# The last two column groups of an encoder block's second MLP product: written order on TensorE in place of the scheduler's

## The chip, the cores and the metric

The kernel runs on one core of a Trainium2 chip. The metric is the device time of one execution in microseconds (us); less is better. Before the change the median of 3 runs is 1791.88 us (1791.26 to 1792.47).

## What is computed

One encoder block on x (256 tokens by 2048 channels), all in float32: two gated branches (chunked gated linear attention and a Hyena convolution), an output projection, a layer norm, then an MLP and a second layer norm. The change touches the MLP's end only:

```python
    h = _layernorm(DEEPNORM_ALPHA * h + mix, ln1_g[l], ln1_b[l])
    ff = jnp.square(jax.nn.relu(h @ w_ff1[l])) @ w_ff2[l]
    h = _layernorm(DEEPNORM_ALPHA * h + ff, ln2_g[l], ln2_b[l])
```

## The kernel before

**Products.** Every float32 operand is split into a high part (rounded to fp32r by ScalarE) and a low part (the remainder, by VectorE: `split_hi_lo`, L89 to L91). A product is three matmuls: high by high, high by low, low by high (L201 to L203 for 512 columns, L969 to L971 for 256). Weights come from DRAM as blocks of 1 MB, `raw`, three buffers; a block is split in two halves of 128x1024.

**The end of the MLP.** The tokens are two blocks of 128, tb 0 and 1; the 2048 output columns are four groups of 512. `ff_pairs` has done most of the k range by another scheme; its sums lie in `z1`. What is left are 10 k tiles (5 half blocks of weights) for each of the 4 column groups and both token blocks, and these run here (from L1373 on):

- Groups 0 and 1: both token blocks together, a half block at a time (w2_30_0 to w2_31_1).
- Group 2 (`left`, PSUM tiles w2_32_0 and w2_32_1) and group 3: their ten half blocks are kept resident, so that token block 0 can go through both groups first and token block 1 afterwards. The first two halves (`kept`) come through the usual buffers, whi and wlo; the other eight are fetched by `resident_pieces` (four loads on L924) into tiles that have come free, in this order: xh_r, xl_r, fraw_r, fa, and four halves of wr3.
- The code writes: 30 products w2_32_0 (tb 0, group 2), 30 products w2_33_0 (tb 0, group 3), then 30 products w2_32_1 (tb 1, group 2), then group 3 of tb 1 in two PSUM tiles of 256 columns, w2_33_10 and w2_33_11, 30 products each.
- `add_ff` (L1360) takes a finished PSUM tile in on VectorE: add to z1 (L1362), two statistics (L1364), and for tb 1 also a multiplication by the gain (L1366).
- After w2_33_0, token block 0 is normed: statistics, `norm_scale`, two chunks on VectorE (L1431, L1441), two on ScalarE (L1433), gain and bias (L1445, L1449), and its four stores on SP (L1418).
- Token block 1's norm is partly done on TensorE: z1 is split (`split_z`, tiles whiz and wloz, the first 1024 columns ahead, 512 more later), multiplied by a unit matrix into PSUM (L1457, six matmuls), and when the last statistics are known (L1463) a diagonal of minus the mean is multiplied with the gain onto it (L1475); then VectorE scales it (L1479) and four stores go out on SP and one on ScalarE's queue.

**Who sets the order.** Instructions of one engine run in the order of its queue. A scheduler that simulates the program in time sets that order from the written program, unless an instruction was handed to `tc.keep_in_program_order`, which puts those instructions of an engine behind one another as written. Before the change that holds for the `ff_pairs` stage (through `pin`) and for VectorE's work from L1440 on and the L1457 matmuls, but not for the products of groups 2 and 3, nor for the splits of the resident blocks.

Of the kernel before, what the change touches and what calls it, by code (L numbers as in the profile page):

```python
# [20 lines left out]
KT = D // P  # L21
# [26 lines left out]
def block_kernel(  # L48
# [25 lines left out]
    nc = tc.nc  # L74
    MM = nc.tensor.matmul

    base = ctx.enter_context(tc.tile_pool(name="base", bufs=1))
# [5 lines left out]
    def psum_main(name):  # L83
        return mmp.tile([P, 512], F32, tag="mm", name=name)
# [4 lines left out]
    def split_hi_lo(hi, lo, src):  # L89
        return (nc.scalar.copy(hi, src),  # L90
                nc.vector.tensor_tensor(lo, src, hi.bitcast(F32), op=ALU.subtract))  # L91
# [20 lines left out]
    def weight_half(n, h):  # L112
        return (wp.tile([P, D // 2], F32R, tag="whi", bufs=3, name=f"whi{n}_{h}"),
                wp.tile([P, D // 2], F32R, tag="wlo", bufs=3, name=f"wlo{n}_{h}"))
# [21 lines left out]
    def next_block():  # L136
        fetch()
        return queue.popleft()
# [50 lines left out]
        for h in range(n, 2):  # L189
            channel_products(ps, act, parts[h], range(8 * h, 8 * h + 8))  # L190

    def token_half(pss, act, half, tbs, kt0, ends=(0, KT - 1)):
        hi, lo = half
        for j in range(2):
            kt = kt0 + j
            wh = hi[:, j * 512:(j + 1) * 512]
            wl = lo[:, j * 512:(j + 1) * 512]
            for tb in tbs:
                sh = act[:, kt, 0, tb * P:(tb + 1) * P]
                sl = act[:, kt, 1, tb * P:(tb + 1) * P]  # L200
                MM(pss[tb], sh, wh, start=(kt == ends[0]), stop=False)  # L201
                MM(pss[tb], sh, wl, start=False, stop=False)  # L202
                MM(pss[tb], sl, wh, start=False, stop=(kt == ends[1]))  # L203

    def token_products(pss, act, blocks, tbs, b0):
        for b, parts in enumerate(blocks):
# [3 lines left out]
    def token_group(act, name):  # L210
        pss = [psum_main(f"{name}_{tb}") for tb in range(NT)]
        for b in range(4):
            token_products(pss, act, [next_block()], range(NT), b)
            pump()
        return pss
# [17 lines left out]
    ident = base.tile([P, P], F32, tag="ident", name="ident")  # L233

    def act_tile(pool, tag, name):
        return pool.tile([P, KT, 2, L], F32R, tag=tag, name=name)
# [5 lines left out]
    dfth = base.tile([P, 4, P], F32R, tag="dfth", name="dfth")  # L242
# [13 lines left out]
    with tc.tile_pool(name="xp", bufs=1) as xp, tc.tile_pool(name="xq", bufs=1) as xq:  # L256
# [44 lines left out]
        for k0, n in PIECES:  # L301
            raw = pieces[k0]
# [12 lines left out]
            if k0 == 0:  # L315
                hi, lo = places[0]
# [165 lines left out]
    for i in range(2 * NCH):  # L482
        c, o = divmod(i, 2)
# [217 lines left out]
    for g in range(4):  # L701
        pss = token_group(xT, f"g1_{g}")
# [168 lines left out]
    for g in range(4):  # L871
        pss = token_group(xT, f"g2_{g}")
# [20 lines left out]
    for g in range(4):  # L893
        pss = token_group(yhT, f"ho{g}")
# [11 lines left out]
    ep = ctx.enter_context(tc.tile_pool(name="ep", bufs=1))  # L906
# [4 lines left out]
    def load_rows(i0):  # L911
        rows = zr[:, 2:4]
        for i in range(2):
            nc.scalar.dma_start(rows[:, i, :], ln_rows[i0 + i:i0 + i + 1, :].broadcast_to([P, D]))
        return rows

    tc.keep_in_program_order(nc.scalar.preload_act_table_set("natural_log_exp_and_others"))

    def resident_pieces(parts):
        for part in parts:  # L920
            n = fetched[0]
            fetched[0] = n + 1
            raw = wp.tile([P, D], F32, tag="raw", bufs=3, name=f"raw{n}")
            nc.sync.dma_start(raw, wblk[n])  # L924
            for h, (hi, lo) in enumerate(part):
                split_hi_lo(hi, lo, raw[:, h * 1024:(h + 1) * 1024])
        return parts

    def resident(slots):
        return resident_pieces([[(hi[:, c:c + 1024], lo[:, c:c + 1024]) for c in (0, 1024)] for hi, lo in slots])  # L930

    def halves(pool, tag, name):
        t = pool.tile([P, 4, D], F32R, tag=tag, name=name)
        return [(t[:, 0], t[:, 1]), (t[:, 2], t[:, 3])]
# [22 lines left out]
        if tb == 0:  # L957
            biased[0] = nc.vector.tensor_tensor(zc, zc, rows[:, 1, at:at + n], op=ALU.add)

    def column_half(pss, act, half, ch, tbs, kt0, ends=(0, KT - 1)):  # L960
        hi, lo = half
        for j in range(2):
            kt = kt0 + j
            cs = slice(j * 512 + ch * 256, j * 512 + ch * 256 + 256)
            for tb in tbs:
                ps = pss[tb][ch][:, 0:256]
                sh = act[:, kt, 0, tb * P:(tb + 1) * P]
                sl = act[:, kt, 1, tb * P:(tb + 1) * P]
                MM(ps, sh, hi[:, cs], start=(kt == ends[0]), stop=False)  # L969
                MM(ps, sh, lo[:, cs], start=False, stop=False)  # L970
                MM(ps, sl, hi[:, cs], start=False, stop=(kt == ends[1]))  # L971

    def column_products(pss, act, blocks, tbs, b0):
        for ch in range(2):
# [9 lines left out]
    for i, t in ((0, turn_b), (1, turn_i)):  # L984
        raw = ep.tile([P, 1024], F32, tag="wx", name=f"turn{i}")[:, 0:512].rearrange("p (a b) -> p a b", b=P)
# [11 lines left out]
    for g in range(3):  # L997
        pss = token_group(mT, f"wo{g}")
# [3 lines left out]
    parts = resident([x0] + halves(ep, "f", "wr1"))  # L1002
    pss = [[psum_main(f"wo3_{tb}{ch}") for ch in range(2)] for tb in range(NT)]
    column_products(pss, mT, [queue.popleft()], range(NT), 0)
    stop_at[0] = FF_PAIRS
    hT = act_tile(ep, "hT", "hT")
# [342 lines left out]
    def ff_close(pss, joins):  # L1349
        form_products(pss, SLOTS - 1, 2, (5, 6))  # L1350
        take_sums(pss, SLOTS - 1, (5, 6))
        for s in range(SLOTS, SLOTS + 8):
            if s in FORMED:
                forms(FORMED[s])
        for j in joins + join_sums(1):
            j()
# [3 lines left out]
    def add_ff(ps, tb, at, n, last=False, order=lambda ins: ins):  # L1360
        zc = z1[:, tb, at:at + n]
        order(nc.vector.tensor_tensor(zc, zc, ps, op=ALU.add))  # L1362
        for i in range(n // 256):
            order(nc.vector.bn_stats(st2[:, tb, at // 256 + i, :], zc[:, i * 256:(i + 1) * 256]))  # L1364
        if tb and not last:
            order(nc.vector.tensor_tensor(zc, zc, rows2[:, 0, at:at + n], op=ALU.mult))  # L1366
# [5 lines left out]
    f3 = Rest()  # L1372
    ENDS = (SLOTS, D_FF // P - 1)  # L1373
# [3 lines left out]
    def next_half():  # L1377
        if not ready:
            ready.extend(next_block())
        return ready.popleft()  # L1380

    for g in range(2):
        pss = [psum_main(f"w2_3{g}_{tb}") for tb in range(NT)]
        for i, kt in enumerate(at_kt):
            token_half(pss, f3, next_half(), range(NT), kt, ENDS)
            if g == 0 and i == 1:
                ff_close(*open_sums)
                rows2 = load_rows(2)
        for tb in range(NT):
            add_ff(pss[tb], tb, g * 512, 512)  # L1390
    left = [psum_main(f"w2_32_{tb}") for tb in range(NT)]
    kept = [next_half() for _ in at_kt[:2]]

    def quarters(*tiles):
        at = [t[:, k:k + 1024] for t in tiles for k in range(0, t.shape[1], 1024)]
        return [[(at[0], at[1]), (at[2], at[3])], [(at[4], at[5]), (at[6], at[7])]]
# [2 lines left out]
    own = [ep.tile([P, n], F32R, tag=t, name=f"{t}_r")  # L1399
           for t, n in (("xh", D), ("xl", D), ("fraw", D))]  # L1400
    parts = resident_pieces(quarters(*own, *spare)
                            + [[(a[:, c:c + 1024], b[:, c:c + 1024]) for c in (0, 1024)] for a, b in halves(ep, "hT", "wr3")])
    parts = [half for block in parts for half in block]
    third, fourth = list(zip(kept + parts[:3], at_kt)), list(zip(parts[3:], at_kt))
    diagonal = base.tile([P, 2, P], F32, tag="as", name="diagonal")
    minus = diagonal[:, 0]
    nc.vector.tensor_scalar(minus, ident, -1.0, None, op0=ALU.mult)
    unit = base.tile([P, 4, P], F32R, tag="dfth", name="unit")[:, 0]
    nc.scalar.copy(unit, ident)
    zg = [weight_half("z", h) for h in range(2)]  # L1410

    def split_z(h, n):
        return split_hi_lo(zg[h][0][:, 0:n], zg[h][1][:, 0:n], z1[:, 1, h * 1024:h * 1024 + n])[1]

    split_z(0, 1024)

    def store(tb, at, n, queue=nc.sync):
        queue.dma_start(out[tb * P:(tb + 1) * P, at:at + n], z1[:, tb, at:at + n])  # L1418

    ps = psum_main("w2_33_0")  # L1420
    for half, kt in third:
        token_half(left, f3, half, [0], kt, ENDS)
    add_ff(left[0], 0, 1024, 512)
    for half, kt in fourth:
        token_half([ps], f3, half, [0], kt, ENDS)
    pss = [psum_main(f"w2_33_1{ch}") for ch in range(2)]
    add_ff(ps, 0, 1536, 512)
    rs, nb = norm_scale(st2, 0, "2")
# [3 lines left out]
    for at, zc, wg, wb in chunks[2:]:  # L1432
        nc.scalar.activation(zc, zc, AF.Identity, scale=rs, bias=nb)  # L1433
    for half, kt in third:
        token_half(left, f3, half, [1], kt, ENDS)
    for ch in range(2):
        for half, kt in fourth:
            column_half([None, pss], f3, half, ch, [1], kt, ENDS)
    keep = tc.keep_in_program_order
    for at, zc, wg, wb in chunks[:2]:  # L1440
        keep(nc.vector.scalar_tensor_tensor(zc, zc, rs, wb, op0=ALU.mult, op1=ALU.add))  # L1441
        store(0, at, 512)
# [35 lines left out]
    for at, n in CENTRED:  # L1478
        nc.vector.scalar_tensor_tensor(z1[:, 1, at:at + n], po[at][:, 0:n], rs, rows2[:, 1, at:at + n],  # L1479
                                       op0=ALU.mult, op1=ALU.add)  # L1480
# [146 lines left out]
```

## Time and profile before

| what | value |
|---|---|
| median of the runs | 1791.88 us |
| the profiled execution's own time | 1790.62 us |
| its span (first to last instruction) | 1788.8 us |
| TensorE matmul busy | 1778.7 us (99%) |
| VectorE busy | 1472.7 us (82%) |
| ScalarE busy | 1050.2 us (59%) |
| granted TensorE clock, mean | 0.999 |

The times below are us from the start of the span. PE is TensorE (PEld its weight loads), DVE VectorE, ACT ScalarE, POOL GpSimd, SP the queue that issues most DMAs. A row of the timeline has start, duration, engine, line, operation, output<-input, and in brackets the idle time of the engine ahead of it with what ended it. The profile leaves out buffer numbers: w2_32_0, w2_33_0 and the others are all `w`, so they are told apart by the order of the queue. Matmuls overlap: a product of 512 columns shows 0.39 us, but the next one starts before it ends.

### The profile page before, as it was taken

Reading aid. Unit: us, or ns where it says so; the run is one execution under the profiler, and the core shown is the slowest. Engines: PE = TensorE matmul, PEld = TensorE weight load, DVE = VectorE, ACT = ScalarE, POOL = GpSimd, SP = SyncE. Lnnn points to the kernel's source line nnn. Section 1 sums busy time; section 2 is a strip of 40 time slices with the busy share of each in tenths; the row PEclk is TensorE's granted clock in tenths of the full one; section 3 lists DMA queues with packets and bytes.
Section 4 is the critical chain, followed back from the end, with each engine's and each line's share of the span. In section 5 each row is a group of like instructions: output and inputs, shape, how many; then the busy total and the mean of one; then the engine's idle time right before and its main releaser. Section 6 shows DMA issues by size and latency. Waiting matters only on the chain.

```text
span 1788.8 us, 23484 instructions
## 1 busy us (share of the span) xinstructions
PE 1778.7 (99%) x8751; PEld 1502.3 (84%) x8751; DVE 1472.7 (82%) x1901; ACT 1050.2 (59%) x1414; POOL 176.9 (10%) x230
## 2 busy tenths in 40 slices
PE   9999999999999999999999999999999999999998
PEld 7888888888888888888888889888888888888886
DVE  6789886885679998998755558889989999999997
ACT  6678777875344444444544446666666666666653
POOL 1011110000011211111000000011111111111100
PEclk9999999999999999999999999999999999999999
DMA  8668775455797979798555674678888888888863
GB/s 320 240 241 294 255 239 200 147 168 203 234 291 244 293 238 289 256 295 259 210 190 183 247 265 153 236 215 267 250 250 253 265 244 265 247 252 254 265 217 135
DMA packets 81010, 427.90 MB, mean 239 GB/s; under 512 B 10008, under 2 KB 12584, under 8 KB 40192
## 3 DMA queue, kind: packets, MB, share of 16 engines
q1 hardware_dynamic: 47664, 336.35, 51.2%
q0 software_dynamic: 26032, 70.13, 19.2%
q10 hardware_dynamic: 7200, 19.93, 3.1%
q8 instruction: 68, 1.11, 0.3%
q14 instruction: 46, 0.38, 0.1%
HBM read 383.43 MB, written 16.25 MB: 223 GB/s over the span
## 4 chain that ended last, share of the span: by engine, by line
PE 98%; DVE 1%; DMA 0%; issue 0%; ACT 0%; SPq 0%; DVEq 0%
PE f L151 13%; PE f L155 7%; PE w L1264 5%; PE w L1266 5%; PE w L1265 5%; PE g L202 3%; PE g L201 3%; PE g L203 3%; PE ux L202 3%; PE ux L203 3%; PE ux L201 3%; PE r L201 2%; PE r L202 2%; PE r L203 2%; PE k L151 2%; PE v L201 2%
## 5 line engine op out<-in xcount | busy, mean ns | idle before, releaser
L90 ACT CAST whi<-raw 128x1024 fp32r<-128x1024 f32 x368 | 387.6, 1055 | 388.4 <-PE ux L203 92.0
L91 DVE TENSOR_TENSOR wlo<-raw,whi 128x1024 fp32r<-128x1024 f32 x368 | 448.3, 1222 | 186.5 <-ACT whi L90 183.4
L151 PE MATMUL f<-hT,whi 128*128 128x512 f32 x984 | 243.6, 391 | 0.0
L151 PEld LDWEIGHTS f<-hT,whi 128*128 128x128 f32 x984 | 180.8, 188 | 35.0
L1122 DVE TENSOR_TENSOR wlo<-fraw,whi 128x1024 fp32r<-128x1024 f32 x108 | 132.0, 1222 | 14.9 <-ACT whi L1125 11.8
L155 PEld LDWEIGHTS f<-hT,wlo 128*128 128x128 f32 x984 | 126.2, 191 | 4.7
L155 PE MATMUL f<-hT,wlo 128*128 128x256 f32 x984 | 127.7, 283 | 0.0
L1125 ACT CAST whi<-ring 128x1024 fp32r<-128x1024 f32 x54 | 56.9, 1054 | 107.0 <-DVE ring L1122 107.0
L1185 POOL DMA_DIRECT2D ring<-wblk x54 | 47.0, 870 | 715.4 <-DVE ring L1122 715.4
L1125 ACT CAST whi<-fraw 128x1024 fp32r<-128x1024 f32 x108 | 113.5, 1051 | 0.1
L202 PE MATMUL g<-wlo,xT 128*128 128x512 f32 x256 | 100.1, 391 | 0.0
L203 PE MATMUL ux<-whi,xT 128*128 128x512 f32 x256 | 99.9, 390 | 0.0
L1125 ACT CAST b_h<-ring 128x1024 fp32r<-128x1024 f32 x108 | 84.9, 835 | 25.5 <-PE w L1266 24.9
L203 PE MATMUL g<-whi,xT 128*128 128x512 f32 x256 | 99.8, 390 | 0.0
L202 PE MATMUL ux<-wlo,xT 128*128 128x512 f32 x256 | 99.6, 389 | 0.0
L201 PE MATMUL g<-whi,xT 128*128 128x512 f32 x256 | 93.8, 392 | 0.0
L201 PE MATMUL ux<-whi,xT 128*128 128x512 f32 x256 | 89.7, 389 | 0.0
L1122 DVE TENSOR_TENSOR b_l<-ring,b_h 128x1024 fp32r<-128x1024 f32 x54 | 66.0, 1221 | 12.8 <-ACT b_h L1125 12.8
L1122 DVE TENSOR_TENSOR ring<-ring 128x512 f32<-128x512 f32 x108 | 74.4, 689 | 1.8
L1122 DVE TENSOR_TENSOR wlo<-ring,whi 128x1024 fp32r<-128x1024 f32 x54 | 66.2, 1225 | 2.5 <-ACT whi L1125 0.6
L1122 DVE TENSOR_TENSOR fa<-ring,fa 128x1024 fp32r<-128x1024 f32 x54 | 65.8, 1219 | 0.0
L1186 POOL DMA_DIRECT2D ring<-ring x54 | 65.2, 1208 | 0.0
(519 smaller groups left out, 4299.6 us busy)
## 6 DMA issues: line engine op xcount, KB each, us to landing
raw<-wblk SPq DMA_DIRECT2D x192, 1024.0 KB, 5.4
fraw<-wblk SPq DMA_DIRECT2D x54, 1024.0 KB, 4.8
ring<-wblk SPq DMA_DIRECT2D x54, 1024.0 KB, 7.2
ring<-wblk POOLq DMA_DIRECT2D x54, 256.0 KB, 4.7
ring<-ring POOLq DMA_DIRECT2D x54, 256.0 KB, 5.6
Td<-T POOLq DMA_DIRECT2D x32, 384.0 KB, 5.4
conv_sb<-conv_rows SPq DMA_DIRECT2D x12, 1024.0 KB, 11.6
Tl<-Td POOLq DMA_DIRECT2D x16, 768.0 KB, 9.2
```

The costliest lines, as they stand in the source:

```text
L90: return (nc.scalar.copy(hi, src), nc.vector.tensor_tensor(lo, src, hi.bitcast(F32), op=ALU.subtract))
L91: nc.vector.tensor_tensor(lo, src, hi.bitcast(F32), op=ALU.subtract))
L151: MM(ps[:, :, ts], hi[:, js], act[:, kt, :, ts], start=(kt == 0 and opens), stop=(kt == KT - 1))
L155: MM(ps[:, 0, ts], lo[:, js], act[:, kt, 0, ts], start=False, stop=False)
L201: MM(pss[tb], sh, wh, start=(kt == ends[0]), stop=False)
L202: MM(pss[tb], sh, wl, start=False, stop=False)
L203: MM(pss[tb], sl, wh, start=False, stop=(kt == ends[1]))
L1122: return pin(nc.vector.tensor_tensor(dst, a, b, op=op))
L1125: return pin(nc.scalar.copy(hi, src))
L1264: pin(MM(ps, sh, wh, start=(p == begin), stop=False))
L1265: MM(ps, sh, wl, start=False, stop=False)
L1266: pin(MM(ps, sl, wh, start=False, stop=(p == end - 1)))
```

## The change

`token_half` and `column_half` get a parameter `order`, through which each of their matmuls goes; for groups 2 and 3 it is `tc.keep_in_program_order`. `resident_pieces` gets the same for the VectorE half of each split. `add_ff` of w2_32_0 is kept in order too, and the first `split_z` is written behind it and kept. The two constants `minus` and `unit` are written ahead of the resident blocks. Nothing is computed otherwise than before.

```diff
-                MM(pss[tb], sh, wh, start=(kt == ends[0]), stop=False)
-                MM(pss[tb], sh, wl, start=False, stop=False)
-                MM(pss[tb], sl, wh, start=False, stop=(kt == ends[1]))
+                order(MM(pss[tb], sh, wh, start=(kt == ends[0]), stop=False))
+                order(MM(pss[tb], sh, wl, start=False, stop=False))
+                order(MM(pss[tb], sl, wh, start=False, stop=(kt == ends[1])))
...
-    def resident_pieces(parts):
+    def resident_pieces(parts, order=lambda ins: ins):
...
-                split_hi_lo(hi, lo, raw[:, h * 1024:(h + 1) * 1024])
+                order(split_hi_lo(hi, lo, raw[:, h * 1024:(h + 1) * 1024])[1])
...
-    split_z(0, 1024)
-
...
     for half, kt in third:
-        token_half(left, f3, half, [0], kt, ENDS)
-    add_ff(left[0], 0, 1024, 512)
+        token_half(left, f3, half, [0], kt, ENDS, keep)
+    add_ff(left[0], 0, 1024, 512, order=keep)
+    keep(split_z(0, 1024))
     for half, kt in fourth:
-        token_half([ps], f3, half, [0], kt, ENDS)
+        token_half([ps], f3, half, [0], kt, ENDS, keep)
...
     for half, kt in third:
-        token_half(left, f3, half, [1], kt, ENDS)
+        token_half(left, f3, half, [1], kt, ENDS, keep)
     for ch in range(2):
         for half, kt in fourth:
-            column_half([None, pss], f3, half, ch, [1], kt, ENDS)
+            column_half([None, pss], f3, half, ch, [1], kt, ENDS, keep)
```

What this moves in the queues. On TensorE, one product of w2_32_0 stood among those of group 1 (w2_31_0 and w2_31_1); a piece of the difference there (without the numbers of the PSUM tiles, w_32_0 is w2_32_0):

```order
 L201 MATMUL w_31_0_14775<-whi_1_14718,fa_9452 128x512
 L201 MATMUL w_31_1_14776<-whi_1_14718,fa_9452 128x512
-L201 MATMUL w_32_0_14844<-whi_0_14748,fa_9302 128x512
 L202 MATMUL w_31_0_14775<-wlo_1_14719,fa_9452 128x512
 L203 MATMUL w_31_0_14775<-whi_1_14718,fa_9452 128x512
```

It now stands at the head of w2_32_0's 30 products, behind all of group 1.

The second place on TensorE is the middle of w2_33_0's products (the last two halves of wr3), before:

```order
L201 MATMUL w2_33_0_14884<-wr3_14849,fa1_9452 128x512
L201 MATMUL w2_32_1_14845<-xl_r_14847,fa1_9452 128x512
L202 MATMUL w2_32_1_14845<-xl_r_14847,fa1_9452 128x512
L203 MATMUL w2_32_1_14845<-xl_r_14847,fa1_9452 128x512
L202 MATMUL w2_33_0_14884<-wr3_14849,fa1_9452 128x512
L203 MATMUL w2_33_0_14884<-wr3_14849,fa1_9452 128x512
```

and after the change the end of w2_33_0, where w2_32_1 begins:

```order
L202 MATMUL w2_33_0_14882<-wr3_14853,fa1_9452 128x512
L203 MATMUL w2_33_0_14882<-wr3_14853,fa1_9452 128x512
L201 MATMUL w2_32_1_14849<-whi300_0_14748,fa0_9302 128x512
L202 MATMUL w2_32_1_14849<-wlo300_0_14749,fa0_9302 128x512
L203 MATMUL w2_32_1_14849<-whi300_0_14748,fa0_9302 128x512
```

Before, 21 of the 30 products of w2_32_1 stood ahead of the last one of w2_33_0 (18 of them from the two kept halves and xh_r, three from xl_r, as above) and 9 behind it; now all 30 stand behind it.

On VectorE the split of z moves, before:

```order
L91 TENSOR_TENSOR fa1_9452<-raw302_14856,fa0_9302 128x1024
L91 TENSOR_TENSOR wr3_14849<-raw303_14862,wr3_14849 128x1024 x2
L91 TENSOR_TENSOR wloz_0_14879<-zr_8507,whiz_0_14878 128x1024
L91 TENSOR_TENSOR wr3_14849<-raw304_14868,wr3_14849 128x1024 x2
L1362 TENSOR_TENSOR zr_8507<-zr_8507,w2_32_0_14844 128x512
L1364 BN_STATS bst2_9308<-zr_8507 128x6 x2
L1362 TENSOR_TENSOR zr_8507<-zr_8507,w2_33_0_14884 128x512
```

and now:

```order
L91 TENSOR_TENSOR fa1_9452<-raw302_14860,fa0_9302 128x1024
L91 TENSOR_TENSOR wr3_14853<-raw303_14866,wr3_14853 128x1024 x2
L91 TENSOR_TENSOR wr3_14853<-raw304_14872,wr3_14853 128x1024 x2
L1362 TENSOR_TENSOR zr_8507<-zr_8507,w2_32_0_14848 128x512
L1364 BN_STATS bst2_9308<-zr_8507 128x6 x2
L91 TENSOR_TENSOR wloz_0_14879<-zr_8507,whiz_0_14878 128x1024
L1362 TENSOR_TENSOR zr_8507<-zr_8507,w2_33_0_14882 128x512
```

wloz has gone behind the two splits of the last block, the addition of w2_32_0 and its statistics. The rest of VectorE's queue, and those of ScalarE, GpSimd and SP, keep their order. In the changed kernel the stores' line is L1417, the two constants' L1393 and L1395, and every line named above from L1441 on has a number less by one.

More of the change, by code (lines that the diff above doesn't have):

```diff
@@ L190, in finish_block, with token_half @@
             channel_products(ps, act, parts[h], range(8 * h, 8 * h + 8))
-    def token_half(pss, act, half, tbs, kt0, ends=(0, KT - 1)):
+    def token_half(pss, act, half, tbs, kt0, ends=(0, KT - 1), order=lambda ins: ins):
         hi, lo = half
@@ L958, in norm_chunk, with column_half @@
             biased[0] = nc.vector.tensor_tensor(zc, zc, rows[:, 1, at:at + n], op=ALU.add)
-    def column_half(pss, act, half, ch, tbs, kt0, ends=(0, KT - 1)):
+    def column_half(pss, act, half, ch, tbs, kt0, ends=(0, KT - 1), order=lambda ins: ins):
         hi, lo = half
@@ L968, in column_half @@
                 sl = act[:, kt, 1, tb * P:(tb + 1) * P]
-                MM(ps, sh, hi[:, cs], start=(kt == ends[0]), stop=False)
-                MM(ps, sh, lo[:, cs], start=False, stop=False)
-                MM(ps, sl, hi[:, cs], start=False, stop=(kt == ends[1]))
+                order(MM(ps, sh, hi[:, cs], start=(kt == ends[0]), stop=False))
+                order(MM(ps, sh, lo[:, cs], start=False, stop=False))
+                order(MM(ps, sl, hi[:, cs], start=False, stop=(kt == ends[1])))
     def column_products(pss, act, blocks, tbs, b0):
@@ L1390, in block_kernel @@
             add_ff(pss[tb], tb, g * 512, 512)
+    diagonal = base.tile([P, 2, P], F32, tag="as", name="diagonal")
+    minus = diagonal[:, 0]
+    nc.vector.tensor_scalar(minus, ident, -1.0, None, op0=ALU.mult)
+    unit = base.tile([P, 4, P], F32R, tag="dfth", name="unit")[:, 0]
+    nc.scalar.copy(unit, ident)
     left = [psum_main(f"w2_32_{tb}") for tb in range(NT)]
+    keep = tc.keep_in_program_order
     kept = [next_half() for _ in at_kt[:2]]
@@ L1401, in block_kernel @@
     parts = resident_pieces(quarters(*own, *spare)
-                            + [[(a[:, c:c + 1024], b[:, c:c + 1024]) for c in (0, 1024)] for a, b in halves(ep, "hT", "wr3")])
+                            + [[(a[:, c:c + 1024], b[:, c:c + 1024]) for c in (0, 1024)] for a, b in halves(ep, "hT", "wr3")], keep)
     parts = [half for block in parts for half in block]
     third, fourth = list(zip(kept + parts[:3], at_kt)), list(zip(parts[3:], at_kt))
[L1405 to L1409, printed above, removed]
     zg = [weight_half("z", h) for h in range(2)]
@@ L1434, in block_kernel @@
     for half, kt in third:
-        token_half(left, f3, half, [1], kt, ENDS)
+        token_half(left, f3, half, [1], kt, ENDS, keep)
     for ch in range(2):
         for half, kt in fourth:
-            column_half([None, pss], f3, half, ch, [1], kt, ENDS)
-    keep = tc.keep_in_program_order
+            column_half([None, pss], f3, half, ch, [1], kt, ENDS, keep)
     for at, zc, wg, wb in chunks[:2]:
```

## The prediction

> **What bounds the kernel now.** First the page: which engine carries the chain that ended last.
>
> ```profile
> PE 98%; DVE 1%; DMA 0%; issue 0%; ACT 0%; SPq 0%; DVEq 0%
> ```
>
> TensorE carries nearly all of it, so a change of order can win only where the chain leaves TensorE. That is in the last 21 us; here is the chain from there on (start, length, engine and line).
>
> ```profile
> 1767.38 0.24 PE w L203
> 1767.64 0.70 DVE zr L1362
> ...
> 1779.10 0.34 DVE zr L1362
> ...
> 1779.93 0.38 DVE mvl L1463
> 1780.34 0.29 DVE diagonal L1468
> ...
> 1780.70 2.84 PE lo L1475 x6
> ...
> 1784.04 0.39 DVEq L1623
> ```
>
> The chain leaves TensorE at 1767.6, when the fourth column group of token block 0 (w2_33_0) is complete, and stays on VectorE until 1780.6. TensorE still has work at 1767.6: it is not the end of its products that sets the end of the kernel, but VectorE's queue behind one of them. So I look at both queues. VectorE first (start, duration, line, in brackets the idle time before it):
>
> ```profile
> 1758.31 2.36 DVE L91 TENSOR_TENSOR wr<-raw,wr 128x1024 fp32r<-128x1024 f32 x2
> 1760.58 0.68 DVE L1362 TENSOR_TENSOR zr<-zr,w 128x512 f32<-128x512 f32 x1
> 1761.30 0.75 DVE L1364 BATCH_NORM_STATS2 bst<-zr 128x6 f32<-128x256 f32 x2
> 1767.64 0.69 DVE L1362 TENSOR_TENSOR zr<-zr,w 128x512 f32<-128x512 f32 x1 [5.60 <-PE w L203]
> ...
> 1771.66 1.41 DVE L1441 SCALAR_TENSOR_TENSOR zr<-zr,lrs 128x512 f32<-128x512 f32 x2
> 1772.99 0.68 DVE L1362 TENSOR_TENSOR zr<-zr,w 128x512 f32<-128x512 f32 x1
> ...
> 1778.43 0.68 DVE L1449 TENSOR_TENSOR zr<-zr 128x512 f32<-128x512 f32 x1
> 1779.02 0.41 DVE L1362 TENSOR_TENSOR zr<-zr,w 128x256 f32<-128x256 f32 x1
> ```
>
> The four additions on L1362 at 1760.58, 1767.64, 1772.99 and 1779.02 take in w2_32_0, w2_33_0, w2_32_1 and the last half group w2_33_11. VectorE is idle for **5.60 us** ahead of the second and then runs without a gap. Now TensorE's queue at the same places:
>
> ```profile
> 1749.09 0.39 PE L203 MATMUL w<-whi,fa 128*128 128x512 f32 x1
> ...
> 1764.95 0.39 PE L202 MATMUL w<-wr,fa 128*128 128x512 f32 x1
> ...
> 1767.22 0.39 PE L203 MATMUL w<-wr,fa 128*128 128x512 f32 x1
> 1767.44 0.39 PE L201 MATMUL w<-xl_r,fa 128*128 128x512 f32 x1
> ...
> 1769.26 0.39 PE L203 MATMUL w<-fraw_r,fa 128*128 128x512 f32 x1
> ...
> 1776.56 0.28 PE L971 MATMUL w<-wr,fa 128*128 128x256 f32 x1
> ...
> 1777.84 0.42 PE L1457 MATMUL lo<-wloz,unit 128*128 128x512 f32 x1
> 1780.68 2.84 PE L1475 MATMUL lo<-zr,diagonal 128*128 128x512 f32 x6 [2.41 <-DVE fin L1469]
> ```
>
> The last product of w2_33_0 starts at 1767.22 and ends at 1767.61 (VectorE starts 0.03 us later), that of w2_32_1 at 1769.26 to 1769.65, that of w2_33_11 at 1776.56 to 1776.84. VectorE takes up w2_32_1 3.34 us late and w2_33_11 **2.18 us late**. At the end TensorE waits 2.41 us for the last statistics. Between those ends, is TensorE ever short of work? Busy time by stretch (TensorE first; PEclk is the granted clock):
>
> ```profile
> 1749.00:1770.00 21.00, 21.00 (x97) 17.45 (x96) 15.27 (x24) 7.37 (x9) 0.00 (x0) 1.00 0.27 103
> 1770.00:1777.00 7.00, 7.00 (x60) 6.96 (x59) 6.79 (x15) 2.24 (x4) 0.00 (x0) 1.00 0.21 75
> ```
>
> It is busy all the time at clock 1.00, so reordering these products can't end them before 1776.84. The tail thus has two limits: VectorE's chain, which sets the end now, and TensorE's stream, 2.18 us less than it.
>
> **What the change moves on TensorE.** The number of instructions, DMAs and queues is the same; only places change. The three groups have 30 products each (5 half blocks, 2 k tiles, 3 products). The row at 1749.09 is the last product of group 1; 89 of the 90 products follow it, the last at 1769.26, so one takes (1769.26 - 1749.09) / 89 = 0.2266 us. The ninetieth stood among those of group 1 (the `-` row in the first piece of the order); it now stands behind them, so that group 1 ends one product earlier and w2_32_0 starts at 1749.09. By the order rows, 21 of w2_32_1's 30 products stood ahead of w2_33_0's last, and all now stand behind it:
> - w2_32_0's 30th product starts at 1749.09 + 29 x 0.2266 = 1755.66, complete at 1756.05. Nothing follows from that: VectorE is at its splits until 1760.58, as before.
> - w2_33_0's last starts at 1749.09 + 59 x 0.2266 = 1762.46, that is 21 x 0.2266 = 4.76 us earlier, complete at 1762.85.
> - w2_32_1's last starts at 1769.26 and w2_33_11's at 1776.56, as before: the same products stand ahead of them.
>
> **Does TensorE now wait for a split?** In the written order each half block is first used earlier, so the cover of its split goes. The rows of the splits, ScalarE's and VectorE's, and the loads behind them (the four issued on L924):
>
> ```profile
> 1748.39 1.22 DVE L91 TENSOR_TENSOR wlo<-raw,whi 128x1024 fp32r<-128x1024 f32 x1
> ...
> 1752.04 1.21 DVE L91 TENSOR_TENSOR fraw_r<-raw,fraw_r 128x1024 fp32r<-128x1024 f32 x1
> ...
> 1753.76 1.22 DVE L91 TENSOR_TENSOR fa<-raw,fa 128x1024 fp32r<-128x1024 f32 x1
> 1754.90 2.35 DVE L91 TENSOR_TENSOR wr<-raw,wr 128x1024 fp32r<-128x1024 f32 x2
> 1757.17 1.22 DVE L91 TENSOR_TENSOR wloz<-zr,whiz 128x1024 fp32r<-128x1024 f32 x1
> ```
> ```profile
> 1757.21 2.00 ACT L90 CAST wr<-raw 128x1024 fp32r<-128x1024 f32 x2 [0.97 <-DMA raw<-wblk]
> ```
> ```profile
> 1748.50 1.47 SPq L924 DMA_DIRECT2D raw<-wblk  x2
> ```
> ```profile
> DMA to landing us min/median/max: 4.8/5.6/7.6
> ```
>
> A half block's low part is first needed by its second product. Its new start against the end of the split:
> - second kept half (product 8): 1749.09 + 7 x 0.2266 = 1750.68; split done 1748.39 + 1.22 = 1749.61; 1.07 us to spare.
> - fraw (product 26): 1754.76 against 1753.25; 1.5 us.
> - fa (32): 1756.11 against 1754.98; 1.1 us.
> - the four halves of wr (38, 44, 50, 56): 1757.47, 1758.83, 1760.19, 1761.55 against about 1756.1, 1757.25, 1759.5, 1760.67; 1.35, 1.6, **0.7** and 0.9 us.
>
> So nothing waits in this execution, and I take zero for stalls. The thin one is the third half of wr: ScalarE's cast waited for its load (the second DMA of the SP row, issued at 1748.50 + 1.47 - 0.33 = 1749.64; the last row has the landings of the four loads on L924, and 1757.21 - 1749.64 is its 7.6). Before, its low product ran at 1764.95, with 5.4 us to spare; that cover is gone. Bounds: nothing from below, and from above a landing as late as the slowest load of this size on the page,
>
> ```profile
> conv_sb<-conv_rows SPq DMA_DIRECT2D x12, 1024.0 KB, 11.6
> ```
>
> 4.0 us later than 7.6, which stalls TensorE by 4.0 - 0.7 = 3.3 us. I take the near end, since the row itself is this very load.
>
> **VectorE.** The split of z (wloz, 1.22 us) moves behind the last two wr splits, the addition of w2_32_0 and its statistics. In its old place VectorE now waits for the first of ScalarE's two casts, which ends at about 1758.2 either way (1757.21 and half of 2.00), so the wr splits keep 1758.31 and the addition 1760.58. Behind them: statistics to 1762.0, wloz to 1763.15, then w2_33_0, complete at 1762.85: the moved split makes that wait 0.3 us. The addition on L1362 starts at 1763.15 in place of 1767.64, **4.49 us earlier**, and L1441 ends at 1773.0 - 4.5 = 1768.5. Now VectorE waits for w2_32_1, to 1769.68: idle 1.2 us, which swallows the 0.3. From there its chain is 1779.02 - 1772.99 = 6.03 us long and would be at the last addition at 1775.71, **3.31 us earlier**; but w2_33_11 is complete only at 1776.84. The last addition starts at about 1776.87 in place of 1779.02: **2.15 us earlier**. wloz itself is needed by the second L1457 product, behind 1776.68: over 13 us to spare.
>
> ScalarE and SP keep their order. ScalarE's two chunks (L1433) and the stores of token block 0 hang on VectorE's chain and come 3.3 to 4.5 us earlier. The two constants that are written earlier (minus, unit) stand at the same places of their queues: nothing. Behind the last addition everything (aggregate, diagonal, the six passes of L1475, scaling, stores) keeps its length: diagonal is ready at 1778.48, and the L1457 products end at 1778.26, so TensorE does not become the bound there.
>
> **Sum.** 1788.8 - 2.15 = 1786.65 span. The profiled execution took 1790.62 with 1.8 us around the span: 1790.62 - 2.15 = 1788.47. It lies 1.26 us under the median of the runs, 1791.88 (1791.26 to 1792.47). For the median: 1791.88 - 2.15 = **1789.7**, 0.12% less.
>
> **Rivals.**
> - **TensorE waits for the late block** (slower). Place: the third wr half's products in w2_33_0. It decides from a landing more than 0.7 us later than 7.6 (gain shrinks), and turns into a loss from 0.7 + 2.15 = 2.85 us later. At the bound above: 3.3 - 2.15 = 1.2 slower, 1793.1; slower by 0.2% (3.6 us) would need a stall of 5.7. For it: the landing of this one is the slowest of its four, and varies. Against: it was issued 1.1 us behind its neighbour and shared the engines with it, which explains the 7.6, and nothing ahead of it moves. [...]
> - **More than TensorE's limit allows.** If the stream of products also ended earlier, VectorE's chain would set the end: 3.31 us, 1788.6, or 4.49 us, 1787.4, if w2_32_1 came earlier too; stores that meet less traffic could add some tenths. Against: 21.00 of 21.00 and 7.00 of 7.00 us busy. What speaks for it is only that ends of matmuls are modelled.
> - **No gain**: the last stores, or some queue that I hold for free, set the end, and the time stays 1791.9 within the spread of the runs. Against: the chain runs through VectorE without an issue gap to 1784.04.
>
> **How the numbers follow.** Forecast 1789.7, with 0.6 of spread and small stalls 1789.1 to 1790.6: 72 in 100. More gain 12 (1787.4 to 1789), of which 9 pass 0.2%; no gain 9 (1790.6 to 1792.5); stall 7 (1791 to 1798), of which 5 are slower by over 0.2%. A measurement of this kernel can tell about 0.2%, 3.6 us, from no change, so the forecast itself counts as within 0.2%. Faster 0.09, same 0.86, slower 0.05. Range 1788.3 to 1792.2: it leaves out half of the second rival, and most of the stalls.
>
> **What would show it.** Right: VectorE's idle ahead of w2_33_0's addition is gone or short, this addition starts near 1763.2, new idle stretches of about 1.2 us ahead of the third and the last addition, both released by TensorE; the wait of L1475 for VectorE shrinks from 2.41 to about 0.3; TensorE still ends L971 at about 1776.8. Wrong: TensorE idle ahead of a wr product (the stall), or L971 ending earlier than 1776.8 (the second rival), or the last addition early and the end not.

## The result, and the profile after

The changed kernel takes 1788.52 us (median of 19 runs, 1787.67 to 1789.95), the kernel before 1791.22 us in 19 runs beside it (1790.26 to 1794.12). The ratio is 0.9984 (95% interval 0.9977 to 0.9991): 2.7 us less by the medians, 1.6 to 4.1 by the interval. 0.2% would be 3.6 us, so by the median the change counts as within 0.2%. The profiled execution took 1788.58 us with a span of 1786.8 us, before 1790.62 and 1788.8.

First the chain that ended last: its shares by engine, and its last pieces (start, length, engine and line; the statistics are L1462 now, the diagonal L1467, the product with it L1474).

```profile
PE 100%; DVE 0%; DVEq 0%; issue 0%
```
```profile
1776.79 0.13 PE w L971
...
1776.95 0.43 DVE zr L1362
...
1777.41 0.44 DVE bst L1364
...
1777.87 0.38 DVE mvl L1462
...
1778.27 0.29 DVE diagonal L1467
...
1778.64 2.84 PE lo L1474 x6
```

Before, the chain left TensorE at 1767.6 and ran on VectorE for 13 us. Now it leaves TensorE at 1776.9, behind the last product of w2_33_11, and VectorE has only the last half group's addition, its statistics and the diagonal to do ahead of the product with the diagonal. VectorE's queue at the places of the prediction (start, duration, line, in brackets the idle time before the row):

```profile
1749.60 1.28 DVE L1362 TENSOR_TENSOR zr<-zr,w 128x512 f32<-128x512 f32 x2
...
1758.36 2.36 DVE L91 TENSOR_TENSOR wr<-raw,wr 128x1024 fp32r<-128x1024 f32 x2 [1.03 <-ACT wr L90]
1760.63 0.68 DVE L1362 TENSOR_TENSOR zr<-zr,w 128x512 f32<-128x512 f32 x1
...
1762.02 1.21 DVE L91 TENSOR_TENSOR wloz<-zr,whiz 128x1024 fp32r<-128x1024 f32 x1
1763.14 0.68 DVE L1362 TENSOR_TENSOR zr<-zr,w 128x512 f32<-128x512 f32 x1
...
1769.76 0.69 DVE L1362 TENSOR_TENSOR zr<-zr,w 128x512 f32<-128x512 f32 x1 [1.20 <-PE w L203]
...
1776.95 0.42 DVE L1362 TENSOR_TENSOR zr<-zr,w 128x256 f32<-128x256 f32 x1 [1.07 <-PE w L971]
```

The idle time of 5.60 us ahead of w2_33_0's addition (now at 1763.14) is gone. In its place VectorE waits 1.20 us for w2_32_1 and 1.07 us for the last half group, both times for TensorE. The first row, group 1's additions, is the mark from which tails are compared below: its start differs by up to 1.6 us between the executions below (1749.35 in dve1_before, 1750.94 in late_block). In before's profile this row is

```profile
1749.52 1.28 DVE L1362 TENSOR_TENSOR zr<-zr,w 128x512 f32<-128x512 f32 x2
```

From mark to last addition it was 1779.02 - 1749.52 = 29.50 us, and is 1776.95 - 1749.60 = 27.35 us: **2.15 us less**. TensorE's rows and its busy time by stretch:

```profile
1762.53 0.39 PE L203 MATMUL w<-wr,fa 128*128 128x512 f32 x1
...
1769.33 0.39 PE L203 MATMUL w<-fraw_r,fa 128*128 128x512 f32 x1
...
1776.63 0.28 PE L971 MATMUL w<-wr,fa 128*128 128x256 f32 x1
...
1778.62 2.84 PE L1474 MATMUL lo<-zr,diagonal 128*128 128x512 f32 x6 [0.32 <-DVE fin L1468]
```
```profile
1749.00:1770.00 21.00, 21.00 (x96) 17.45 (x95) 18.53 (x32) 8.97 (x11) 0.00 (x0) 1.00 0.33 124
1770.00:1777.00 7.00, 7.00 (x60) 6.96 (x59) 5.79 (x12) 0.62 (x1) 0.00 (x0) 1.00 0.17 64
```

w2_33_0's last product starts at 1762.53 in place of 1767.22; those of w2_32_1 and w2_33_11 stay where they were (1769.33 and 1776.63, 0.07 later like the whole tail). TensorE never waits for a split, and its wait ahead of the product with the diagonal shrinks from 2.41 to 0.32 us.

### The profile page after: what moved, and what is told of

Same layout as the page of the kernel before. It is cut to its first block, busy times and chain, and to the rows that moved or that the text cites. A ratio compares the mean times of both kernels' runs of the same rounds, so it can differ in the third digit from the quotient of the medians.

```text
span 1786.8 us, 23484 instructions
## 1 busy us (share of the span) xinstructions
PE 1779.6 (100%) x8751; PEld 1502.9 (84%) x8751; DVE 1473.1 (82%) x1901; ACT 1049.5 (59%) x1414; POOL 176.5 (10%) x230
## 4 chain that ended last, share of the span: by engine, by line
PE 100%; DVE 0%; DVEq 0%; issue 0%
PE f L151 13%; PE f L155 7%; PE w L1264 5%; PE w L1266 5%; PE w L1265 5%; PE g L202 3%; PE g L201 3%; PE g L203 3%; PE ux L202 3%; PE ux L203 3%; PE ux L201 3%; PE r L201 2%; PE r L203 2%; PE r L202 2%; PE k L151 2%; PE v L202 2%
```

## The experiments

Each run stands beside runs of the kernel before on the same chip; a ratio is to these. The first four ask which engine sets the end: work is added to one engine, on either kernel, at a place where it delays nothing but what that engine does next.

**Nine more products of 512 columns on TensorE** (9 x 0.2266 = 2.04 us), ahead of the two halves of the last group, in the changed kernel (pe9_after) and in the kernel before (pe9_before):

```diff
+    pad = psum_side("pad")
+    for _ in range(9):
+        keep(MM(pad, f3[:, SLOTS, 0, 0:P], third[0][0][0][:, 0:512], start=True, stop=True))
     for ch in range(2):
         for half, kt in fourth:
```

> The changed kernel with nine extra products of 512 columns on TensorE (into a PSUM tile that nothing reads), put in among the first products of w2_33_10, ahead of w2_33_11. Nothing is left out. My theory: in the changed kernel TensorE's stream sets the end, so the extra 9 x 0.2266 = 2.04 us are paid in full: 2.0 us slower than the changed kernel, about 0.6 us faster than the kernel before, and VectorE's wait ahead of the last addition grows from 1.07 to about 2 us. Rival (something behind TensorE sets the end, such as stores): under 0.5 us slower than the changed kernel.

> The kernel before with the same nine extra products at the same place of TensorE's queue. My theory: there VectorE's chain sets the end, and TensorE has 2.18 us to spare at w2_33_11, so the extra 2.04 us cost nothing: within 0.2 us of the kernel before, the last addition still near 1779.0 and not released by TensorE. Rival (TensorE's stream has set the end all along): 2.0 us slower than the kernel before.

Measured: pe9_after 1790.91 us, ratio 0.9999 (0.999 to 1.0008); pe9_before 1790.92 us, ratio 0.9997 (0.9988 to 1.0006). VectorE's mark and last addition, of pe9_after and then of pe9_before:

```profile
1749.69 1.28 DVE L1362 TENSOR_TENSOR zr<-zr,w 128x512 f32<-128x512 f32 x2
...
1779.08 0.42 DVE L1362 TENSOR_TENSOR zr<-zr,w 128x256 f32<-128x256 f32 x1 [2.12 <-PE w L971]
```
```profile
1750.52 1.27 DVE L1362 TENSOR_TENSOR zr<-zr,w 128x512 f32<-128x512 f32 x2
...
1780.01 0.41 DVE L1362 TENSOR_TENSOR zr<-zr,w 128x256 f32<-128x256 f32 x1
```

29.39 us from mark to last addition against 27.35: the changed kernel pays 2.04 us, all of it. 29.49 against 29.50: the kernel before pays nothing, the products fill the time in which TensorE waited (0.41 us are left of the 2.41 ahead of the product with the diagonal). By the medians pe9_after is level with the kernel before (1790.91 against 1790.89) and not the expected 0.6 us under it; a difference of that size lies inside the interval.

**Two more VectorE additions of 128x512** ahead of the last one, in the changed kernel (dve2_after) and before (dve2_before), and later one more in before (dve1_before, the same with range(1)):

```diff
+    extra = ep.tile([P, 1024], F32, tag="wx", name="extra")[:, 0:512]
...
+            for _ in range(2):
+                keep(nc.vector.tensor_tensor(extra, wg, wb, op=ALU.add))
```

> The changed kernel with two extra additions of 128x512 on VectorE (about 0.65 us each, into a tile that nothing reads) between the additions of w2_33_10 and w2_33_11. My theory: they fill the 1.07 us that VectorE waits ahead of the last addition, so of 1.3 us only about 0.2 are paid; the last addition starts near 1777.2 with no idle ahead of it. Rival (VectorE's chain still sets the end): 1.3 us slower than the changed kernel.

> The kernel before with the same two extra additions on VectorE at the same place. My theory: VectorE's chain sets the end there, so they are paid in full, 1.3 us slower than the kernel before, last addition near 1780.3. Rival (TensorE's stream sets the end): nothing.

Measured: dve2_after 1789.05 us, ratio 0.9988 (0.9979 to 0.9997); dve2_before 1793.29 us, ratio 1.0011 (1.0002 to 1.002). The last additions, of dve2_after and of dve2_before:

```profile
1750.35 1.28 DVE L1362 TENSOR_TENSOR zr<-zr,w 128x512 f32<-128x512 f32 x2
...
1777.87 0.41 DVE L1362 TENSOR_TENSOR zr<-zr,w 128x256 f32<-128x256 f32 x1
```
```profile
1749.96 1.28 DVE L1362 TENSOR_TENSOR zr<-zr,w 128x512 f32<-128x512 f32 x2
...
1780.78 0.41 DVE L1362 TENSOR_TENSOR zr<-zr,w 128x256 f32<-128x256 f32 x1
```

27.52 against 27.35: the changed kernel pays 0.17 us, the rest fits into the idle time that stood at 1.07. 30.82 against 29.50: the kernel before pays 1.32, as its theory had it. So VectorE's chain set the end before, and TensorE's stream sets it now. But the median of dve2_before rose by 2.4 us and not by 1.3. Its row of the product with the diagonal, and the stretch ahead of it (PEclk is the third number from the end):

```profile
1782.43 5.49 PE L1478 MATMUL lo<-zr,diagonal 128*128 128x512 f32 x6 [3.73 <-DVE fin L1472]
```
```profile
1781.00:1784.00 3.00, 1.57 (x2) 0.84 (x3) 2.44 (x9) 0.85 (x3) 0.00 (x0) 0.54 0.22 87
```

The six products take 5.49 us in place of 2.84, because the granted clock is at half: 0.50 from 1781.26 on (the stretch above begins 0.26 us before that) until 1788.08. That had no place in the expectation, and is followed up below.

**Each half of the change alone.** products_only undoes VectorE's half, vector_only TensorE's; changed_again is the changed kernel once more, beside them.

```diff
-                            + [[(a[:, c:c + 1024], b[:, c:c + 1024]) for c in (0, 1024)] for a, b in halves(ep, "hT", "wr3")], keep)
+                            + [[(a[:, c:c + 1024], b[:, c:c + 1024]) for c in (0, 1024)] for a, b in halves(ep, "hT", "wr3")])
...
+    split_z(0, 1024)
...
-    add_ff(left[0], 0, 1024, 512, order=keep)
-    keep(split_z(0, 1024))
+    add_ff(left[0], 0, 1024, 512)
```

> The changed kernel without its VectorE half: products in written order, but the splits of the resident blocks, the addition of w2_32_0 and the split of z left to the scheduler. In VectorE's queue the addition of w2_32_0, its statistics and the split of z then stand ahead of the splits of the last two wr halves (about 2.5 us of work, of which 1 us lay idle there). My theory: the low part of the third wr half is ready at about 1760.9 in place of 1759.5, against a use at 1760.2: TensorE waits some 0.6 us for it, then perhaps a tenth more at the fourth; the end moves by as much: 0.6 us slower than the changed kernel, still about 1.5 to 2 us faster than before. Rival (the order of the splits is what brings the gain): no gain over the kernel before. Second rival (the splits' order does nothing): same as the changed kernel, no idle on TensorE.

```diff
-        token_half(left, f3, half, [0], kt, ENDS, keep)
+        token_half(left, f3, half, [0], kt, ENDS)
...
-            column_half([None, pss], f3, half, ch, [1], kt, ENDS, keep)
+            column_half([None, pss], f3, half, ch, [1], kt, ENDS)
```

> The changed kernel without its TensorE half: the splits, the addition of w2_32_0 and the split of z in written order on VectorE, the products left to the scheduler, which gives nearly the queue of before; only three products of w2_32_1 go from ahead of w2_33_0's last to behind it. My theory: w2_33_0 is complete 3 x 0.2266 = 0.7 us earlier and VectorE's unbroken chain with it, so 0.7 us faster than the kernel before, the addition of w2_33_0 near 1767.0. Rival (the splits' order brings the gain): the whole 2 to 2.7 us. Second rival: nothing.

> The changed kernel once more, beside the three above on the same chip. My theory: 2.15 us less than the kernel before, with the last addition released by TensorE. If it gains 2.7 us again, some 0.5 us of it are not in my sum.

Measured: products_only 1789.67 us, ratio 0.999 (0.9981 to 0.9999); vector_only 1790.46 us, ratio 0.9996 (0.9987 to 1.0004); changed_again 1789.39 us, ratio 0.9987 (0.9978 to 0.9996), a gain of 1.8 us by the medians. The trace of changed_again has 27.36 us from mark to last addition, and TensorE releases that addition, as in the profile above. From products_only the one row of TensorE that waits for a split, and from vector_only w2_33_0's addition and the mark ahead of it:

```profile
1760.20 0.39 PE L201 MATMUL w<-wr,fa 128*128 128x512 f32 x1
1761.12 0.50 PE L202 MATMUL w<-wr,fa 128*128 128x512 f32 x1 [0.53 <-DVE wr L91]
```
```profile
1750.22 1.27 DVE L1362 TENSOR_TENSOR zr<-zr,w 128x512 f32<-128x512 f32 x2
...
1767.66 0.69 DVE L1362 TENSOR_TENSOR zr<-zr,w 128x512 f32<-128x512 f32 x1 [3.98 <-PE w L203]
```

The written order of the products brings the gain, and VectorE's half protects it: from mark to last addition products_only takes 28.19 us, 1.31 less than before, where the whole change takes 2.15 less. Without VectorE's half, the addition of w2_32_0, two statistics and wloz stand ahead of the last two wr splits. These start 10.10 us after the mark in place of 8.76, that is 1.34 later, and the cover of 0.7 us that the prediction called thin is used up. The third half of wr comes late for its second product: 1761.12 - 1760.20 = 0.92 us between two starts in place of 0.23, and 0.34 to the next one, so 0.80 us of the stream. VectorE's half alone moves 3 of w2_32_1's products behind w2_33_0: its addition comes 17.44 us after the mark instead of 1767.64 - 1749.52 = 18.12, 0.68 us = 3 x 0.2266, and the last addition 0.69 us earlier (28.81).

**A late block.** The last weight block is loaded twice, so that the price of the rival could be read (late_block); then only its first 256 columns a second time (late_quarter), for a short wait.

```diff
-            nc.sync.dma_start(raw, wblk[n])
+            for _ in range(2 if n == nblk - 1 else 1):
+                nc.sync.dma_start(raw, wblk[n])
```

> The changed kernel with the load of the last weight block issued twice into the same buffer, the second behind the first, so that its halves come some 5 us later. Queues are otherwise the same. My theory (a landing more than 0.7 us later stalls TensorE one for one): landing near 1762.1 in place of 1757.3, the cast to 1763.2, the low part to 1764.4 against a use at 1760.3: TensorE idle some 4.2 us in two pieces ahead of the third wr half, the end 4.2 us later, about 1.5 us slower than the kernel before. [...] Rival (the block's landing is still hidden): as fast as the changed kernel.

```diff
             nc.sync.dma_start(raw, wblk[n])
+            if n == nblk - 1:
+                nc.sync.dma_start(raw[:, 0:256], wblk[n, :, 0:256])
```

> The changed kernel, with a second load of the first 256 columns behind the last weight block's own load; the output stays the same. Theory: the piece that waits for it comes about 2 us later than TensorE's turn, TensorE waits in one or two short pieces of about 1 us each, the granted clock stays at 1.00, and the end comes later by the wait alone: about 2.1 us over the changed kernel, level with the kernel before, TensorE's pitch staying at 0.227 us a product behind the wait. Rival: a wait in pieces also takes the clock down, as the one of 3.17 us did in late_block, and the end comes 4 us or more later than that of the changed kernel. Third: the load is done sooner than the two rows of late_block say and nothing is to be seen.

Measured: late_block 1795.14 us, ratio 1.0022 (1.0012 to 1.0031), 5.75 over changed_again; late_quarter 1790.46 us, ratio 0.9995 (0.9986 to 1.0004). TensorE's rows at the wait, of late_block (with the granted clock in the stretches around it) and of late_quarter:

```profile
1761.15 0.39 PE L203 MATMUL w<-wr,fa 128*128 128x512 f32 x1
1764.71 0.80 PE L201 MATMUL w<-wr,fa 128*128 128x512 f32 x1 [3.17 <-ACT wr L90]
1765.97 0.80 PE L202 MATMUL w<-wr,fa 128*128 128x512 f32 x1 [0.47 <-DVE wr L91]
1766.56 0.63 PE L203 MATMUL w<-wr,fa 128*128 128x512 f32 x1
...
1770.83 0.56 PE L201 MATMUL w<-whi,fa 128*128 128x512 f32 x1
1771.23 0.40 PE L202 MATMUL w<-wlo,fa 128*128 128x512 f32 x1
```
```profile
1761.00:1764.00 3.00, 0.54 (x3) 0.12 (x1) 0.00 (x0) 0.39 (x1) 0.00 (x0) 1.00 0.62 259
1764.00:1771.00 7.00, 5.83 (x13) 4.26 (x14) 4.84 (x6) 1.60 (x2) 0.00 (x0) 0.53 0.00 0
1771.00:1773.00 2.00, 2.00 (x10) 1.62 (x9) 1.83 (x5) 0.01 (x1) 0.00 (x0) 0.96 0.00 0
```
```profile
1760.12 0.39 PE L203 MATMUL w<-wr,fa 128*128 128x512 f32 x1
1761.17 0.50 PE L201 MATMUL w<-wr,fa 128*128 128x512 f32 x1 [0.66 <-ACT wr L90]
1762.43 0.50 PE L202 MATMUL w<-wr,fa 128*128 128x512 f32 x1 [0.76 <-DVE wr L91]
1762.77 0.39 PE L203 MATMUL w<-wr,fa 128*128 128x512 f32 x1
```

In late_block ten products from 1766.56 to 1770.83 start 0.427 us apart, where 0.227 is usual: +2.0 us behind a wait of which the first two starts had already cost 3.33 + 1.03 us. With 0.5 us more on the two products at the edges the stream loses 6.9 us. In late_quarter the four starts lie 2.65 us apart instead of 0.68, +1.97, and the clock stays at 1.00 behind it: two short waits cost no more than themselves, about 2 us in the trace from mark to last addition (29.34 against 27.36) and 1.1 by the medians, which were taken on different chips.

The profiled execution of late_block is one of its longer ones (1796.86 us against a median of 1795.14). By the medians 5.75 us are lost, 1.4 more than the 4.36 of the two waiting starts; the half clock's share thus differs from execution to execution (the mean granted clock of the nine runs is 0.997 to 0.999).

**From what wait on the clock falls.** dve1_before makes TensorE's wait in the kernel before a little longer:

> The kernel before, with one further VectorE addition of 128x512 (0.65 us) in the tail; the output stays the same. Theory: VectorE sets the end of the kernel before, so the addition is paid in full, +0.65 us in the trace; TensorE's idle time ahead of the product with the diagonal grows from 2.41 to about 3.05 us and the six products stay at 2.84 us. Rival: 3.05 us of idle time is already enough to take the clock down as 3.73 us did in dve2_before (products 5.49 us, VectorE then waits 0.93 us): about +1.6 us or more.

Measured: 1792.63 us, ratio 1.0007 (0.9998 to 1.0016). The mechanism of the rival held; by the medians it costs 1.2 us and not 1.6 or more. From mark to last addition it takes 30.09 us, 0.59 more than before, as the theory had it, but the wait is 3.02 us and the six products take 4.51:

```profile
1781.10 4.51 PE L1478 MATMUL lo<-zr,diagonal 128*128 128x512 f32 x6 [3.02 <-DVE fin L1472]
```

The clock fell to 0.50 only 1.0 us after work had begun again (at 1782.13), and it was back at 1.00 3.41 us later. That, with late_block and dve2_before, made a theory on the kernel before itself, tried by two more profiles of it, without an edit:

> The kernel before, unchanged, profiled once more. In the traces so far the granted clock changes only at points 3.41 us apart (in dve1_before at 1782.13 and 1785.55, in late_block at 1764.35 and, two such stretches later, 1771.12), and it fell behind stretches of 3.41 us in which TensorE was idle for 2.38, 2.56 and 2.81 us, not behind one with 1.76 (vector_only). In the profile of before the 2.41 us of idle time fell across two stretches, 1.69 and 0.73. Theory: where the stretches begin differs from execution to execution, so in some executions of the kernel before the 2.41 us lie in one stretch, and the clock falls: by the two bounds in 1.06 to 2.3 of 3.41 cases, that is 31 to 67 in 100. Then the six products of 2.84 us take 4 us or more, VectorE's scaling waits for them, and the span is about 1.3 us longer, as in dve1_before. Rival: 2.41 us of idle time never takes the clock down, and the products take 2.84 us in each profile. Seen in neither of two looks, the theory would have had 11 to 48 in 100 to look so, and it stays open.

> The second look at the kernel before, with the same theory and rival: 31 to 67 in 100 for six products of 4 us or more and a wait in VectorE's scaling, or 2.84 us. In either case the point at which the clock falls behind the last product, less whole multiples of 3.41 us, tells how the 2.41 us lay: the theory asks for a fall where at least 2.38 us of it were in one stretch, and for none where 1.76 us or less were.

Measured: 1790.74 us and 1792.34 us, one execution each. The product with the diagonal, and TensorE's busy time in stretches of 3.41 us laid from the points at which the clock changed, of before_look_1 and then of before_look_2:

```profile
1780.77 2.84 PE L1475 MATMUL lo<-zr,diagonal 128*128 128x512 f32 x6 [2.41 <-DVE diagonal L1468]
```
```profile
1775.73:1779.14 3.41, 2.63 (x17) 1.98 (x15) 3.34 (x8) 0.26 (x1) 0.00 (x0) 1.00 0.20 77
1779.14:1782.56 3.42, 1.79 (x4) 0.87 (x5) 3.14 (x11) 1.07 (x3) 0.00 (x0) 1.00 0.20 77
```
```profile
1781.32 4.54 PE L1475 MATMUL lo<-zr,diagonal 128*128 128x512 f32 x6 [2.41 <-DVE fin L1469]
```
```profile
1777.98:1781.39 3.41, 1.00 (x5) 0.45 (x3) 3.27 (x10) 0.38 (x2) 0.00 (x0) 1.00 0.40 154
1781.39:1784.80 3.41, 3.41 (x4) 1.40 (x5) 1.80 (x5) 0.84 (x2) 1.26 (x1) 0.50 0.00 0
1784.80:1788.21 3.41, 1.06 (x3) 0.19 (x1) 1.63 (x3) 0.00 (x0) 0.00 (x0) 1.00 0.89 301
```

The wait is 2.41 us in both. In the first it lies across two stretches, TensorE is busy for 2.63 and 1.79 us of them, and the clock stays. In the second it lies in one stretch, with 1.00 us busy; the clock is at half for exactly the next stretch, and the products take 1.70 us more. The span, set against before's by the mark (1750.16 here), is 1790.6 - 1788.8 - 0.64 = 1.2 us longer. The theory held.

How often it happens is known by the bounds (31 to 67 in 100), by one of the three profiles of the kernel before, and by the mean granted clock that every run's record gives, rounded to 0.001. Half rate for one stretch of 3.41 us takes 3.41 x 0.5 / 1790 = 0.001 off this mean. Of the 85 runs of the kernel before that stand beside the experiments, 20 show 0.998, as before_look_2 does, and the others 0.999; on the three chips those 20 took 0.7 to 1.2 us more in the mean than the others. It is 0.998 in 9 of 11 runs of dve2_before and 6 of 11 of dve1_before, and in none of the 30 runs of the changed kernel, none of the 11 of pe9_before (wait 0.41 us) and none of the 11 of vector_only (wait 1.76 us). Because of the rounding 20 of 85 is a lower bound: the profiled execution of dve1_before had the half clock and shows 0.999.

## Why the prediction was right, and where not

- **What bounds the kernel**: right. VectorE's chain set the end before (dve2_before's last addition 1.32 later, pe9_before's not at all), TensorE's stream does after (pe9_after pays 2.04 of 2.04, dve2_after 0.17).
- **The move on TensorE**: right. w2_33_0's last product was put at 1762.46 and stands at 1762.53, with the whole tail 0.07 later; the ends of w2_32_1 and w2_33_11 did not move.
- **No wait for a split**: right, and the margin of 0.7 us was real. products_only overran it and waited.
- **VectorE**: right. w2_33_0's addition was forecast at 1763.15 and is at 1763.14, the new wait at 1.2 us and is 1.20; the last addition at 1776.87 and is at 1776.95.
- **The sum**: 2.15 us less from mark to last addition, as forecast; the own time of the profiled execution was forecast at 1788.47 and is 1788.58.
- **From there to the median**: the forecast of 1789.7 is 1.2 us over the 1788.52 measured. That lies inside the range, but by 0.2 us only, and outside the band of 1789.1 to 1790.6 that had 72 in 100; it falls in the band given to more gain (12 in 100), whose mechanism did not occur. So the mechanism and the 2.15 us were right, and that the range still held the median is in part luck: its low end was set for another rival. 0.66 of that is the base: before's median of three runs was 1791.88, of nineteen 1791.22. The other 0.55 is what the medians give over 2.15. The step "For the median: 1791.88 - 2.15" carries the gain of one execution to all, and the profiled one was an execution in which the wait of 2.41 us did not cost the clock. In before_look_2 the same wait cost 1.2 us on top, and with 0.32 us left the changed kernel can't pay it. A share of 31 to 67 in 100 of 1.2 us is an estimate of 0.4 to 0.8 us of mean gain, so 2.5 to 3.0 in all. That fits 2.7, but the two measures of the changed kernel, 2.7 and 1.8, lie too far apart to prove it. The granted clocks of the runs without a profile show that the mechanism is at work there too, in at least 20 of 85 runs of the kernel before and in none of the changed one; how much of the 0.55 it explains stays open.
- **The stall rival**: did not occur, and its price was mis-sized. In late_block the second load landed 4.97 us behind the first; the prediction's rule (landing less 0.7) gives a wait of 4.27, and 3.33 + 1.03 = 4.36 was lost at the two waiting products. What the 1793.1 lacks is the half clock behind the wait (3.17 us in late_block), +2.5 us in the profiled execution, where two stretches of 3.41 us ran at 0.50, and 1.4 by the medians. At the bound itself, a stall of 3.3 us, no run was made, and no run shows what would fill the stall's range up to 1798; late_block's nine runs, with 4.36 us at the two waiting products, took 1793.7 to 1797.3 us. Nor is the 2.41 us, the longest idle time of TensorE in before's tail, safe: in before_look_2 the clock fell to 0.50 behind it.
- **No gain** and **more than TensorE's limit allows**: neither is seen; 21.00 of 21.00 and 7.00 of 7.00 us stay busy, and the stores follow the earlier end.

## What to carry to other kernels

Where two engines both nearly set the end, look for the one with a single idle stretch and no gap behind it: what feeds the end of that stretch is what to move, and the gain ends where the other engine's stream ends, however much more the chain would give. Price a wait of TensorE by more than its length: here one of 1.76 us (vector_only) left the clock at 1.00 behind it, one of 2.41 us halved it in before_look_2 and not in before_look_1, and those of 3.02 us (dve1_before), 3.17 (late_block) and 3.73 (dve2_before) halved it, so take the profile of a kernel with such a wait more than once before a sum is made from it. Order the producers (here the splits) as well as the consumers: the order of the products alone came with a wait of 0.5 us, which cost 0.8 us of the tail and which the written order of VectorE's splits took away.

## What the runs showed of the hardware

- In these traces the granted clock changes only at points 3.41 us apart (or a multiple of it), which lie differently in each execution: half rate from 1782.13 to 1785.55 in dve1_before, from 1781.39 to 1784.80 in before_look_2, from 1764.35 to 1771.18 (twice 3.41) in late_block.
- A stretch need not be idle throughout for the clock to fall behind it: it fell behind stretches with 1.00 and 1.06 us of work in them (both before_look_2), and stayed behind one with 1.65 us (vector_only, a wait of 1.76 us):

```profile
1778.76:1782.17 3.41, 1.65 (x5) 0.77 (x5) 3.13 (x11) 0.77 (x3) 0.00 (x0) 1.00 0.20 77
```

The ends of the traces narrow it: the clock fell behind 1.36 us of work (vector_only, 1782.17 to 1785.58) and stayed behind 1.50 (late_block, 1788.24 to 1791.66). So in these traces the limit lies between 1.36 and 1.50 us of work in 3.41, that is 2.05 to 1.91 us without. The reckoning of before_look_1 (in what share of positions enough of a wait of 2.41 us lies in one stretch) then gives (3.41 - 2.41 + 2 x (2.41 - 2.05)) / 3.41, 50 in 100, to 59 in 100, an estimate.

- One stretch full of work brought the clock back (before_look_2, 1781.39 to 1784.80), and so did one with 3.25 us (dve2_before, 1784.67 to 1788.08); one with 2.59 of 3.41 us busy (late_block, 1764.35 to 1767.76) did not.
- 1.7 us more in the products at the end cost only 1.2 us of span (before_look_2). The issue of the four stores on SP that follow takes 3.06 us there and 2.18 in before; whether that has to do with the difference was not tested.
